# A two-layer decoder trunk on one core: tiles shifted so that matmul operands begin at multiples of 512 bytes, and the order inside the attention heads changed

## The chip, the core and the metric

The kernel runs on one core of a Trainium2 chip, and the metric is the device time of one execution in microseconds. The engines work side by side: TensorE (PE in the profile; its weight loads are a row of their own, PEld), VectorE (DVE), ScalarE (ACT), GpSimd (POOL) and SyncE (SP), which issues DMAs. On-chip memory has 128 partitions. A tile takes the same range of bytes in each of its partitions, so every tile has a first byte in its partition, and every operand of a matmul begins at some byte there. A matmul has two operands: the **moving** one, whose columns stream through the array, and the **stationary** one, which a weight load puts into the array beforehand. In the profile's rows `acc<-xTh,w` names the output, then the moving, then the stationary tile.

## What is computed

512 tokens of width 1024 pass through two layers. The reference, cut to its frame:

```python
for i in range(DEPTH):
    if i % 2 == 0:
        m = hybrid_attention_mixer(x, ...)   # latent attention (8 heads) + block attention (8 heads)
    else:
        m = ssd_mixer(x, ...)                # state-space mixer, 32 heads in 4 groups
    x = layer_norm(DEEPNORM_ALPHA * x + m, ln_mix_g[i], ln_mix_b[i])
    f = conv_ffn(x, w_up, conv_w, conv_b, w_down)      # width 2816, gated
    x = layer_norm(DEEPNORM_ALPHA * x + f, ln_ffn_g[i], ln_ffn_b[i])
    x = x + jax.nn.sigmoid(x @ ple_w_gate[i]) * (p[i] @ ple_w_proj[i])
```

All values are float32. In the latent attention a head's key is 64 columns of its own and 32 rotary columns that all eight heads share.

## The kernel before

**Arithmetic.** Each float32 operand of a large product is split into a high part (rounded to a matmul format, by ACT) and the rest (by DVE): `split`, lines 71 to 76. `mm3` (lines 104 to 107) then issues three matmuls for each product: high by high (L105), high by low (L106), low by high (L107). They have 128 stationary columns and mostly 512 moving ones. A weight is loaded by a DMA on SP's queue into `raw` (three buffers), split into a `w` tile, and used once.

**Streams.** Nearly all of the time is a few long streams of `mm3`. In the up projections of the feed-forward layers and the input projections of the mixer (`up_a`, `proj_a`) the weights are stationary and the transposed activations `xTh`, `xTl` move: `acc<-xTh,w`. In the down projections the weights move and the hidden tiles `h` are stationary: `acc<-w,h`. The state-space mixer's output has `acc<-w,yT`; the gate of the per-layer embedding has `pg<-w,xTh`, with its weights in the pool `hp`. In the attention output the half from block attention is `wo<-w,ob` and the half from latent attention `om<-w,om`: the same loop over the same shapes, with the weights of `wo` in the pool `wp` and those of `om` in `qkp`.

**Where tiles begin.** Pools take their room in the order in which they are opened, and a pool's tiles follow each other. The tiles of one pool are multiples of 512 bytes long (2,048, 4,096, 16,384), so all of them begin at the same remainder of 512, which comes from the small constants and statistics laid before them; and slices for matmuls step in multiples of 512 bytes. In the kernel before, `rawp`, `wp`, `xp`, `sp` and `tp` (weights `w`, tokens, scratch, `xTh`, `xTl`) have remainder 96; `c4`, `qkp`, `ptp`, `prp`, `big` and `hp` (keys and queries, `cT`, `pT`, `ob`, `om`, `h`, the weights of `pg` and `om`) have 224; `two`, `three` and `cvp` of the mixer (`yT`, `xdt`, `state`) have 64. So the two operands of a matmul begin at: `acc<-xTh,w` 96 and 96; `acc<-w,h` and `wo<-w,ob` 96 and 224; `pg<-w,xTh` 224 and 96; `om<-w,om` 224 and 224; `acc<-w,yT` 96 and 64.

**The heads.** The sixteen heads run as eight pairs, p = 0 to 7, the latent ones from p = 4. PE's order there is written by hand: at each p two pieces of `scores` (L329, tile `s`), then `turn` of the pair before (transposes of its weights, L356, tile `pt`), then `values` (L368, tile `o`); the table `between` puts other products into four gaps. `kr_step` makes the shared rotary key, `c_transpose` and `c_split` the split latent vectors `cT`, `v_step` (`vm`) and `uq_step` (`uq`) values and queries, and `ready` a pair's keys and queries (`mla_k`: `mk`, `mla`: `mq`). A scheduler that simulates the engines orders ACT, DVE, POOL and SP; `issue_after` holds a block of its work behind a named instruction.

Of the kernel before, what the change touches and what calls it, by code (L numbers as in the profile page):

```python
# [10 lines left out]
F32 = mybir.dt.float32  # L11
F32R = mybir.dt.float32r
I32 = mybir.dt.int32
AF = mybir.ActivationFunctionType
# [19 lines left out]
def trunk(ctx, tc, I, out):  # L34
# [9 lines left out]
    def pool(name, bufs, **kw):  # L44
        return ctx.enter_context(tc.tile_pool(name=name, bufs=bufs, **kw))
# [7 lines left out]
    st = pool("st", 4)  # L53
    pa = [pool(f"pa{i}", 2, space=PSUM) for i in range(2)]
# [16 lines left out]
    def split(h, l, src, eng=V, hi=A):  # L71
        if hi is A:
            A.activation(h, src, AF.Copy)  # L73
        else:
            hi.tensor_copy(h, src)
        eng.tensor_tensor(l, src, h.bitcast(F32), op=OP.subtract)  # L76
# [37 lines left out]
    qg = cp.tile([P, 3], F32, name="qg")  # L114

# [158 lines left out]
    def attention():  # L274
        with ExitStack() as es:
# [208 lines left out]
            def mla_k(j):  # L484
                ps = acc("mk", 1)
                w = L["wkv"][0][:, :, j * P:(j + 1) * P]
                mm3(ps, w[:, 0], w[:, 1], cT[2][:, 0], cT[2][:, 1], True, True)
                for x in range(2):
                    y = qkp.tile([P, 2, 512], F32R, tag="qk", name="mk")
                    split(y[0:64, 0], y[0:64, 1], ps[64 * x:64 * x + 64])  # L490
                    nc.scalar.dma_start(y[64:96].bitcast(F32), L["kr"].bitcast(F32))
                    mk[2 * j + x] = y
# [27 lines left out]
            def pj_load(half, *pools):  # L520
                L["pj"] = PleProj([(0, half)], *pools)
# [19 lines left out]
            def ready(p):  # L541

                if p >= 4:
# [9 lines left out]
                       3: ([(pp, 0, 0, 2), (pp, 0, 0, 3)], [(ct, 2), (ct, 0), (ct, 1), (kr_step,), (cs, 2), (cs, 0), (cs, 1)],  # L553
                           [(uq_load, 1), (vm, 0), (uq, 0, 0)],
                           [(uq, 0, 1), (uq, 0, 2), (uq, 0, 3), (vm, 1), (vm, 2), (uq, 1, 0), (ready, 4), (vm, 3)]),
                       4: ([(uq, 1, 1), (out_load, 0)], [(uq, 1, 2)], [(ready, 5), (uq, 1, 3)],
# [202 lines left out]
    def ssd(xs, xT):  # L759
        with ExitStack() as es:  # L760
# [6 lines left out]
            cvp = lpool("cvp", 2)  # L767
            cw = one.tile([P, 24, 5], F32, name="scw")
# [256 lines left out]
            ones = one.tile([P, P], F32, name="ones")  # L1025
            G.memset(ones, 1.0)
            b2 = bank("le")
            T.matmul(b2[:, :P], ones, da, start=True, stop=True)
# [121 lines left out]
```

## Time and profile before

| | us |
|---|---|
| median of 3 runs | 1468.15 (1464.94 to 1468.96) |
| the profiled execution | 1466.06 |
| its span, first to last instruction | 1464.3 |
| PE busy | 1452.5 |
| DVE busy | 855.5 |
| ACT busy | 656.4 |

The span is the time from the first instruction to the last; 1.8 us of the profiled execution lie around it. A matmul's own duration in the rows holds the filling and draining of the array and overlaps that of the next; what a matmul costs in a stream is the distance from its start to the next start.

### The profile page before, as it was taken

Reading aid. Unit: us, or ns where it says so; the run is one execution under the profiler, and the core shown is the slowest. Engines: PE = TensorE matmul, PEld = TensorE weight load, DVE = VectorE, ACT = ScalarE, POOL = GpSimd, SP = SyncE. Lnnn points to the kernel's source line nnn. Section 1 sums busy time; section 2 is a strip of 40 time slices with the busy share of each in tenths; the row PEclk is TensorE's granted clock in tenths of the full one; section 3 lists DMA queues with packets and bytes.
Section 4 is the critical chain, followed back from the end, with each engine's and each line's share of the span. In section 5 each row is a group of like instructions: output and inputs, shape, how many; then the busy total and the mean of one; then the engine's idle time right before and its main releaser. Section 6 shows DMA issues by size and latency. Waiting matters only on the chain.

```text
span 1464.3 us, 19196 instructions
## 1 busy us (share of the span) xinstructions
PE 1452.5 (99%) x7264; PEld 1194.8 (82%) x7264; DVE 855.5 (58%) x1499; ACT 656.4 (45%) x1273; POOL 138.1 (9%) x235
## 2 busy tenths in 40 slices
PE   9999999999999999999999999999999999999998
PEld 7876878888888888889888788787888888888887
DVE  5367787545445334756576877768854445423472
ACT  5476654534343322345756565463354333322331
POOL 2133313000000000100121201112100000000010
PEclk9999999999999999999999999999999999999999
DMA  6304133332333233332434333433333333232511
GB/s 236 112 30 155 59 112 110 101 101 92 97 100 101 89 99 129 131 118 76 140 109 130 103 114 108 130 108 116 96 117 95 97 101 101 87 101 86 174 49 51
DMA packets 51932, 155.93 MB, mean 106 GB/s; under 512 B 6400, under 2 KB 13312, under 8 KB 51840
## 3 DMA queue, kind: packets, MB, share of 16 engines
q1 hardware_dynamic: 39168, 135.49, 29.1%
q10 hardware_dynamic: 12672, 19.21, 4.1%
q8 instruction: 57, 0.93, 0.3%
q14 instruction: 35, 0.29, 0.1%
HBM read 148.26 MB, written 5.37 MB: 105 GB/s over the span
## 4 chain that ended last, share of the span: by engine, by line
PE 96%; DVE 2%; ACT 1%; DMA 1%; issue 0%; ACTq 0%; SPq 0%
PE acc L105 25%; PE acc L106 25%; PE acc L107 25%; PE pg L107 2%; PE pg L106 2%; PE pg L105 2%; PE s L329 2%; PE intra L915 1%; PE xTb L136 1%; PE pt L356 1%; PE o L368 1%; PE state L929 1%; PE inter L915 1%; PE wo L105 1%; PE om L105 1%; PE wo L107 1%
## 5 line engine op out<-in xcount | busy, mean ns | idle before, releaser
L76 DVE TENSOR_TENSOR w<-raw,w 128x512 fp32r<-128x512 f32 (+1 forms) x438 | 297.4, 689 | 282.1 <-ACT w L73 281.6
L73 ACT ACTIVATE w<-raw 128x512 fp32r<-128x512 f32 (+1 forms) x438 | 268.4, 625 | 403.0 <-PE acc L107 354.1
L106 PE MATMUL acc<-xTl,w 128*128 128x512 f32 (+1 forms) x1104 | 413.8, 375 | 0.8 <-DVE xTl L76 0.8
L105 PE MATMUL acc<-xTh,w 128*128 128x512 f32 (+1 forms) x1104 | 413.5, 376 | 0.2 <-ACT xTh L73 0.2
L107 PE MATMUL acc<-xTh,w 128*128 128x512 f32 (+1 forms) x1104 | 413.0, 374 | 0.0
L106 PEld LDWEIGHTS acc<-xTl,w 128*128 128x128 f32 x1104 | 207.9, 188 | 38.3 <-DVE xTl L76 1.2
L107 PEld LDWEIGHTS acc<-xTh,w 128*128 128x128 f32 x1104 | 207.8, 188 | 37.4 <-issue 0.6
L105 PEld LDWEIGHTS acc<-xTh,w 128*128 128x128 f32 x1104 | 207.4, 188 | 38.0 <-issue 1.1
L106 PE MATMUL acc<-w,h 128*128 128x512 f32 x352 | 139.1, 395 | 0.0
L107 PE MATMUL acc<-w,h 128*128 128x512 f32 x352 | 138.7, 395 | 0.0
L105 PE MATMUL acc<-w,h 128*128 128x512 f32 x352 | 138.5, 395 | 0.0
L607 DVE SCALAR_TENSOR_TENSOR conv<-acc,cw,conv 128x511 f32<-128x511 f32 x88 | 65.7, 746 | 87.2 <-ACT conv L605 87.2
L127 POOL TENSOR_TENSOR mv<-rs,half_neg 128x1 f32<-128x1 f32 x16 | 13.9, 869 | 760.8 <-DVE rs L126 760.8
L106 PEld LDWEIGHTS acc<-w,h 128*128 128x128 f32 x352 | 66.3, 188 | 15.5
L105 PEld LDWEIGHTS acc<-w,h 128*128 128x128 f32 x352 | 66.3, 188 | 15.3
L107 PEld LDWEIGHTS acc<-w,h 128*128 128x128 f32 x352 | 66.3, 188 | 15.3
L605 ACT ACTIVATE conv<-acc,cw 128x512 f32<-128x512 f32 x44 | 34.3, 780 | 83.6 <-PE acc L107 83.6
L631 DVE TENSOR_TENSOR conv<-conv,acc 128x512 f32<-128x512 f32 x44 | 30.3, 688 | 59.8 <-PE acc L107 57.3
L607 DVE SCALAR_TENSOR_TENSOR cv<-acc,scw,cv 128x511 f32<-128x511 f32 (+2 forms) x72 | 53.4, 744 | 15.4 <-ACT cv L605 14.8
L106 PE MATMUL pg<-w,xTh 128*128 128x512 f32 (+1 forms) x136 | 52.2, 384 | 0.0
L105 PE MATMUL pg<-w,xTh 128*128 128x512 f32 (+1 forms) x136 | 52.1, 384 | 0.0
L107 PE MATMUL pg<-w,xTl 128*128 128x512 f32 (+1 forms) x136 | 52.1, 383 | 0.0
(287 smaller groups left out, 2042.3 us busy)
## 6 DMA issues: line engine op xcount, KB each, us to landing
raw<-in_w_up SPq DMA_DIRECT2D x88, 512.0 KB, 3.5
raw<-in_w_down SPq DMA_DIRECT2D x44, 512.0 KB, 3.5
raw<-in_w_xbc SPq DMA_DIRECT2D x24, 512.0 KB, 3.5
raw<-in_w_ple_gate SPq DMA_DIRECT2D x16, 512.0 KB, 4.6
raw<-in_w_z SPq DMA_DIRECT2D x16, 512.0 KB, 3.5
lab<-rows ACTq DMA_DIRECT2D x16, 512.0 KB, 5.3
raw<-in_w_sout SPq DMA_DIRECT2D x16, 512.0 KB, 3.5
raw<-in_w_qkv SPq DMA_DIRECT2D x11, 512.0 KB, 4.9
```

What stands on the lines that cost most here:

```text
L73: A.activation(h, src, AF.Copy)
L76: eng.tensor_tensor(l, src, h.bitcast(F32), op=OP.subtract)
L105: T.matmul(ps, lh, rh, start=start, stop=False)
L106: T.matmul(ps, lh, rl, start=False, stop=False)
L107: T.matmul(ps, ll, rh, start=False, stop=stop)
L136: T.transpose(b[:, k * P:(k + 1) * P], src[:, (half * 4 + k) * P:(half * 4 + k + 1) * P], ident)
L329: T.matmul(b[:, :e], q[:, ts], k[:, :e], start=n == 0, stop=n == len(qk) - 1)
L356: T.transpose(b[:, at:at + P], self.soft[x][2][i][:, t], ident)
L605: A.activation(f, ps, AF.Identity, bias=cw[:, taps:taps + 1], scale=cw[:, taps - 1:taps])
L607: V.scalar_tensor_tensor(f[:, k:], ps[:, :S - k], cw[:, taps - 1 - k:taps - k], f[:, k:], op0=OP.mult, op1=OP.add)
L631: V.tensor_tensor(g, g, pu, op=OP.mult)
L915: T.matmul(b[64 * x:64 * x + 64, k * P:(k + 1) * P], weights[:, h * 64:h * 64 + 64], moving(h), start=True, stop=True)
```

## The change

Three tiles that only take room are added (384 bytes behind the pool `st`, 416 among the constants, 128 in the mixer's pool `one`), each written once by POOL, and the mixer's `ones` shrinks from 128 to 8 columns, with a piece of scratch filled with ones in its place for one matmul. With that, `rawp`, `wp`, `xp`, `sp`, `tp`, `c4`, `qkp`, `ptp`, `prp`, `big`, `hp`, `two`, `three` and `cvp` all begin at a multiple of 512. The identity that moves in every transpose stays at remainder 128, and the column sums of the mixer's norm (`ss`) stay off a multiple.

In the heads, `kr_step` goes ahead of the `cT` transposes; one more `vm` is computed earlier and the last one later; in `mla_k` both high parts are issued before both low parts; and the load and split of the second embedding projection (`pj_load`) are held until the end of the transposes of pair 5.

```diff
+    G.memset(pool("pad", 1).tile([P, 96], F32, name="pad"), 0.0)
...
+    G.memset(cp.tile([P, 104], F32, name="pad0"), 0.0)
...
-                for x in range(2):
-                    y = qkp.tile([P, 2, 512], F32R, tag="qk", name="mk")
-                    split(y[0:64, 0], y[0:64, 1], ps[64 * x:64 * x + 64])
+                halves = [ps[64 * x:64 * x + 64] for x in range(2)]
+                ys = [qkp.tile([P, 2, 512], F32R, tag="qk", name="mk") for _ in range(2)]
+                for y, h in zip(ys, halves):
+                    A.activation(y[0:64, 0], h, AF.Copy)
+                for x, (y, h) in enumerate(zip(ys, halves)):
+                    V.tensor_tensor(y[0:64, 1], h, y[0:64, 0].bitcast(F32), op=OP.subtract)
                     nc.scalar.dma_start(y[64:96].bitcast(F32), L["kr"].bitcast(F32))
                     mk[2 * j + x] = y
...
             def pj_load(half, *pools):
-                L["pj"] = PleProj([(0, half)], *pools)
+                with tc.issue_after(pairs[5].last_a.ins) if half else ExitStack():
+                    L["pj"] = PleProj([(0, half)], *pools)
...
-                       3: ([(pp, 0, 0, 2), (pp, 0, 0, 3)], [(ct, 2), (ct, 0), (ct, 1), (kr_step,), (cs, 2), (cs, 0), (cs, 1)],
-                           [(uq_load, 1), (vm, 0), (uq, 0, 0)],
-                           [(uq, 0, 1), (uq, 0, 2), (uq, 0, 3), (vm, 1), (vm, 2), (uq, 1, 0), (ready, 4), (vm, 3)]),
-                       4: ([(uq, 1, 1), (out_load, 0)], [(uq, 1, 2)], [(ready, 5), (uq, 1, 3)],
+                       3: ([(pp, 0, 0, 2), (pp, 0, 0, 3)], [(kr_step,), (ct, 2), (ct, 0), (ct, 1), (cs, 2), (cs, 0), (cs, 1)],
+                           [(uq_load, 1), (vm, 0), (vm, 1), (uq, 0, 0)],
+                           [(uq, 0, 1), (uq, 0, 2), (uq, 0, 3), (vm, 2), (uq, 1, 0), (ready, 4), (uq, 1, 1)]),
+                       4: ([(uq, 1, 2), (out_load, 0)], [(vm, 3)], [(ready, 5), (uq, 1, 3)],
...
+            G.memset(one.tile([P, 32], F32, name="pads"), 0.0)
...
-            ones = one.tile([P, P], F32, name="ones")
+            ones = one.tile([P, 8], F32, name="ones")
             G.memset(ones, 1.0)
+            all_ones = w0[:, :P]
+            G.memset(all_ones, 1.0)
             b2 = bank("le")
-            T.matmul(b2[:, :P], ones, da, start=True, stop=True)
+            T.matmul(b2[:, :P], all_ones, da, start=True, stop=True)
```

What stands on DVE behind the scores of p = 3, where PE's next transposes wait for DVE's copies of `pt`. Before:

```order
L445 TENSOR_SCALAR cg<-ct,qg 128x512 x3
L75 CAST spare<-kr 32x512
L361 COPY pt<-pt 128x512
L76 TENSOR_TENSOR cT<-cg,cT 128x512 x2
L76 TENSOR_TENSOR spare<-kr,spare 32x512
L361 COPY pt<-pt 128x512
L76 TENSOR_TENSOR cT<-cg,cT 128x512
L76 TENSOR_TENSOR pT<-p_raw,pT 128x512
L361 COPY pt<-pt 128x512
```

After, on DVE at the same place:

```order
L77 CAST spare<-kr 32x512
L448 TENSOR_SCALAR cg<-ct,qg 128x512
L78 TENSOR_TENSOR spare<-kr,spare 32x512
L448 TENSOR_SCALAR cg<-ct,qg 128x512 x2
L364 COPY pt<-pt 128x512
L78 TENSOR_TENSOR cT<-cg,cT 128x512
L364 COPY pt<-pt 128x512
L78 TENSOR_TENSOR cT<-cg,cT 128x512
L364 COPY pt<-pt 128x512
```

Both roundings of the shared key (`spare<-kr`) now stand ahead of the first copy, one `cT` instead of two and a key behind it, and the split of `pT` is gone from here.

What stands on DVE between the weights of pair 4 and the scores of p = 5, where PE waits for the keys and queries `mk` and `mq` of pair 5. Before:

```order
L76 TENSOR_TENSOR mk<-mk 64x512
L76 TENSOR_TENSOR w<-raw,w 128x512
L76 TENSOR_TENSOR pT<-p_raw,pT 128x512
L76 TENSOR_TENSOR w<-raw,w 128x512
L76 TENSOR_TENSOR mk<-mk 64x512
L76 TENSOR_TENSOR mq<-mq 96x512 x2
L76 TENSOR_TENSOR ob<-o,ob 128x512
```

After, on DVE at the same place:

```order
L497 TENSOR_TENSOR mk<-mk 64x512 x2
L78 TENSOR_TENSOR mq<-mq 96x512 x2
L78 TENSOR_TENSOR w<-raw,w 128x512
L78 TENSOR_TENSOR ob<-o,ob 128x512
L335 ISA pr,nmx<-s,mask 128x512
```

The three weight and embedding splits no longer stand between the two keys; one weight split is left, behind the queries. On ACT the two `mk` rows stand together too, with the DMA of the shared key behind them.

## Rows read from the trace of the kernel before

**Rows 1.** The page: busy time by engine; the chain that ended last, by engine.

```profile
PE 1452.5 (99%) x7264; PEld 1194.8 (82%) x7264; DVE 855.5 (58%) x1499; ACT 656.4 (45%) x1273; POOL 138.1 (9%) x235
...
PE 96%; DVE 2%; ACT 1%; DMA 1%; issue 0%; ACTq 0%; SPq 0%
```

**Rows 2.** Windows: stretch, length, PE busy (instructions), clock, DMA share, GB/s.

```profile
280.00:380.00 100.00, 100.00 (x443) 1.00 0.30 95
...
490.00:590.00 100.00, 100.00 (x432) 1.00 0.37 121
```

**Rows 3.** Groups by line and shape: count | busy us, mean ns | idle before.

```profile
L105 PE MATMUL acc<-xTh,w 128*128 128x512 f32 x944 | 369.1, 391 | 0.0
...
L105 PE MATMUL acc<-w,h 128*128 128x512 f32 x352 | 138.5, 395 | 0.0
...
L105 PE MATMUL acc<-w,yT 128*128 128x512 f32 x128 | 51.1, 399 | 0.0
...
L105 PE MATMUL pg<-w,xTh 128*128 128x512 f32 x120 | 47.6, 398 | 0.0
```

**Rows 4.** Timeline of PE, up projection: start us, duration us, instruction.

```profile
299.80 0.39 PE L105 MATMUL acc<-xTh,w 128*128 128x512 f32 x1
...
302.07 0.39 PE L106 MATMUL acc<-xTl,w 128*128 128x512 f32 x1
```

**Rows 5.** Timeline of PE, down projection.

```profile
500.06 0.40 PE L105 MATMUL acc<-w,h 128*128 128x512 f32 x1
...
503.55 0.39 PE L105 MATMUL acc<-w,h 128*128 128x512 f32 x1
```

**Rows 6.** Timeline of PE, gate of the embedding, 512 columns.

```profile
640.20 0.39 PE L105 MATMUL pg<-w,xTh 128*128 128x512 f32 x1
...
642.30 0.40 PE L105 MATMUL pg<-w,xTh 128*128 128x512 f32 x1
```

**Rows 7.** Timeline of PE, output of the state-space mixer.

```profile
1026.12 0.39 PE L106 MATMUL acc<-w,yT 128*128 128x512 f32 x1
...
1030.79 0.39 PE L105 MATMUL acc<-w,yT 128*128 128x512 f32 x1
```

**Rows 8.** Timeline of PE, the two halves of the attention output.

```profile
161.53 0.39 PE L105 MATMUL wo<-w,ob 128*128 128x512 f32 x1
...
164.08 0.39 PE L107 MATMUL wo<-w,ob 128*128 128x512 f32 x1
...
214.82 0.39 PE L106 MATMUL om<-w,om 128*128 128x512 f32 x1
...
216.40 0.39 PE L107 MATMUL om<-w,om 128*128 128x512 f32 x1
```

**Rows 9.** Timeline of PE, last gate, 256 columns.

```profile
1454.82 0.28 PE L105 MATMUL pg<-w,xTh 128*128 128x256 f32 x1
...
1458.06 0.28 PE L105 MATMUL pg<-w,xTh 128*128 128x256 f32 x1
```

**Rows 10.** Waits of PE: waiting line <- releaser: us in total, times, longest.

```profile
PE s L329 <- ACT mq L73: 1.6, 2, 1.1
PE pt L356 <- ACT pt L359: 1.4, 1, 1.4
...
PE s L329 <- DVE mq L76: 0.7, 1, 0.7
PE pt L356 <- DVE pt L361: 0.5, 1, 0.5
```

**Rows 11.** Timelines of ACT and DVE in the heads, p = 3 to 5.

```profile
125.31 1.65 ACT L73 ACTIVATE cT<-cg 128x512 fp32r<-128x512 f32 x3
...
127.16 0.67 DVE L76 TENSOR_TENSOR spare<-kr,spare 32x512 fp32r<-32x512 f32 x1
...
156.65 0.68 DVE L76 TENSOR_TENSOR pT<-p_raw,pT 128x512 fp32r<-128x512 f32 x1
```

**Rows 12.** Windows, all engines, the middle of the heads: PE clock before DMA share.

```profile
100.00:146.00 46.00, 42.30 (x233) 32.69 (x232) 34.92 (x95) 31.19 (x79) 15.59 (x44) 0.96 0.37 123
```

**Rows 13.** Timeline at the start: POOL's memsets, PE's first stream.

```profile
0.73 0.52 POOL L287 MEMSET zero<- 128x512 f32 x1 [0.29 <-POOLq L1142]
1.19 0.42 POOL L119 MEMSET mask<- 128x384 f32 x1
...
5.52 0.50 PE L105 MATMUL acc<-w,xTh 128*128 128x512 f32 x1
```

## The prediction

> **What bounds the kernel now.** I read the page first: PE is busy for 99% of the span and holds 96% of the chain that ended last [rows 1]. Whatever is not on PE therefore counts only where PE waits for it. The waits of PE by name come next: those of the heads are 1.6, 1.4, 0.7 and 0.5 us [rows 10], and nothing comparable stands in the long streams. So the change can bring time in two ways only: fewer PE waits in the heads, or a shorter distance from one matmul's start to the next in the streams.
>
> The second is what the shifted tiles touch, so I looked for streams of equal shape with different distances. The windows show it at once: 100 us of up projection hold 443 matmuls, 100 us of down projection 432, both with the clock at 1.00 of its upper level, 2.4 GHz, and PE busy throughout [rows 2]. The timelines give the distances of matmuls with 512 moving and 128 stationary columns. Up projection: 10 starts in 2.27 us, 227.0 ns [rows 4]. Down projection: 15 in 3.49 us, 232.7 ns [rows 5]. Gate: 9 in 2.10 us, 233.3 ns [rows 6]. State-space output: 20 in 4.67 us, 233.5 ns [rows 7].
>
> Set beside where the operands begin (moving, stationary): 96 and 96 costs 227.0; 96 and 224 costs 232.7; 224 and 96 costs 233.3; 96 and 64 costs 233.5. These streams differ in more than that, so the pair that decides is the attention output, one loop over equal shapes whose two halves differ in the pool of the weights. `wo` (96 and 224) takes 11 starts in 2.55 us, 231.8 ns; `om` (224 and 224) takes 7 in 1.58 us, 225.7 ns, within the rounding of two starts the 227 of the up projection [rows 8]. **My reading:** a stream is short where both operands begin at the same remainder of 512, whichever that is, and 5 to 6.5 ns longer where they don't. After the change all of them begin at 0 and 0, which the trace does not show.
>
> **The change part by part. The shifted tiles.** If 0 and 0 behaves as 96 and 96 and as 224 and 224, the slow streams come to 227.0. Each of the counts stands for three lines [rows 3]:
> - down projections: 3 × 352 = 1,056 matmuls by 232.7 − 227.0 = 5.7 ns: 6.0 us;
> - state-space output: 384 by 6.5 ns: 2.5 us;
> - gates: 360 by 6.3 ns: 2.3 us;
> - `wo`: 96 by 4.8 ns: 0.5 us.
>
> The rest with unequal starts (`uq`, `vm`, some of `pj`; under 300, partly narrower) would give at most 1.5 us at the same rate; I take 0.5. The sum is 11.8 us, all on PE in streams in which it waits for nothing, so all of it is on the path. ACT and DVE are busy for 45% and 58% of the span [rows 1], so a stream 2.5% faster should not be starved.
>
> The bounds of the unknown, what 0 and 0 costs: the nearest rows are the two equal pairs (227.0 and 225.7 by rounding), which give nothing off or up to a nanosecond for all streams, and the three unequal ones (up to 233.5), which would be a loss. I take 227.0, because two different equal pairs lie there, and no row of an equal pair lies at 232. Below, a floor comes from the narrow gate: with 256 columns, 27 starts take 3.24 us, 120.0 ns [rows 9]. From 256 to 512 columns a matmul of the equal pairs thus grows by 107 ns, so 512 columns alone are 214 ns and 13 ns are a fixed part, whose origin no row tells.
>
> The Trainium skill ("TensorE: Matmul & The Clock Gate", Step-by-step: what each phase is for) says that PE reads SBUF through two independent read ports, one for the streaming operand and one for the weights. By that rule two operands could not get into each other's way, where they begin would be without effect, and only the heads would gain (the second rival). The trace speaks against it: `wo` and `om` differ by 6 ns with nothing else changed [rows 8].
>
> **The heads.** PE's order is by hand, so I follow who waits for whom. Pair 5: the scores `s` wait for ACT's and DVE's `mq` because DVE works on two weight splits and one split of `pT` between the two `mk` (the order rows; the `pT` split is 0.68 us [rows 11]), and ACT's second `mk` waits behind the same splits. With these gone the keys and queries are ready about 2 us sooner, more than the waits. Pair 4: ACT's second `mk` follows the first at once, and two `uq` products in place of one `vm` cover more of the wait. Both waits of `s`, 1.6 + 0.7 us [rows 10], go: −2.3 us. What comes late next is PE itself.
>
> Ahead of that, at p = 3, the picture is mixed. The first copy of `pt` on DVE now stands behind one more split of the shared key (0.67 us [rows 11]), so the transposes that waited 0.5 us wait up to 0.6 us longer. ACT's copy stands behind two `cT` instead of three (1.65 us for three [rows 11]), which takes some 0.5 us off the 1.4 us wait. I count it as zero, with +0.6 and −1.4 as ends. In this stretch the granted clock is 0.96 [rows 12], which is 4% of 46 us, 1.8 us, at most to be had back if PE's pause no longer lets it fall to 1.2 GHz; I take none, and +0.9 as the other end, if the pause gets longer. Sum of the heads: −2.3, between −5.5 and +1.5.
>
> `pj_load` is held until the transposes of pair 5 are through. What waits for it are the last `pj` products, behind the attention output; two splits of `pT` and the weight splits move into the pairs 6 and 7, where DVE and ACT are free between the pieces. SP's queue gets one load of `raw` later; no weight of pair 6 is behind it. Zero, and 0.7 us if one split should hold a PE step.
>
> **The added memsets.** Two stand ahead of the zero fill that starts PE's warm-up. The 512-column fill starts 0.46 us before the next one [rows 13]; two of about a fifth of that are 0.2 us. PE's first stream, at 5.52 us, follows right on the warm-up, so I add 0.1 (0 to 0.25). The fill of ones for the mixer is one POOL step in a stretch where POOL is idle (9% busy [rows 1]): zero.
>
> **Sum.** 1466.1 − 11.8 − 2.3 + 0.1 = 1452.1 for an execution like the profiled one, which is 2.1 us under the median of the runs; against the median that is **1454**.
>
> **The rivals.**
> 1. *The fixed part goes too.* The 13 ns beyond the columns might be what it costs that operands begin off some boundary: all streams of before begin at 96, 224 or 64, never at 0. The four streams of rows 3 hold 3 × (944 + 352 + 128 + 120) = 4,632 matmuls; half to all of 13 ns is 30 to 60 us more, 1424 to 1394. For it: nothing in the trace begins at 0. Against it: 96, 224 and 64 are three different remainders, and the fixed part is never smaller than in the equal pairs. The Trainium skill ("TensorE: Matmul & The Clock Gate", Back-to-back issue gap) gives a warm distance of N / 2.4 + 2.5 ns, 215.8 ns for 512 columns, without a word on where operands begin; by it, as an estimate from that page, 11.2 ns would go and the time would be near 1402. No row of before reaches it.
> 2. *The place does not matter.* The streams differ for another reason (which tile is stationary, which engine wrote it last), and only the heads change: 1466.1 − 2.2 + 2.1 = 1466. The pair `wo` and `om` speaks against it.
> 3. *Equal starts at 0 collide.* Slower: if both operands begin in the same place of the 512 bytes and that place is the bad one, the up projections and their like, 3 × 944 = 2,832 matmuls at 227.0, go to the 233.5 of the slowest pair: +18.4 us, while the slow streams stay: 1466.1 + 18.4 − 2.2 + 2.1 = 1484. It decides from the distance at which the streams together break even with all that is gained: (11.3 − 0.5 + 2.2) / 4,632 = 2.8 ns above 227.0, so from 229.8 ns on. Against it: two equal pairs, both short.
>
> **How the numbers follow.** The forecast 58%, rival 1 17%, rival 2 13%, rival 3 12%. 0.3% of the time, 4.4 us, is about what a measurement of this kernel can tell from no change: 1463.8 to 1472.6 counts as the same. Forecast and rival 1 are faster: 0.75; rival 2 is the same: 0.13; rival 3 is slower: 0.12. The forecast's own range is 1446 to 1464: streams 1 ns shorter than 227.0 (about 5 us) with 3 us more from the heads, to streams 1 ns longer with the heads at their bad end. The range reaches up to the other cases, 1446 to 1486, and leaves out rival 1.
>
> **What would show it.** In the profile after: 100 us of down projection should hold as many matmuls as 100 us of up projection, 443, and the gate and state-space output should start every 227 ns (right), all streams at 216 to 222 (rival 1), the differences unchanged (rival 2), or all near 233 (rival 3). The waits of `s` for `mq` should be gone from the list, those of `pt` stay at about 2 us, and the clock of the middle of the heads at 0.96 or above. I am wrong altogether if the distance depends on something that the tiles' shift changes besides the remainder, such as which tiles are neighbours.

## The result and the profile after

The changed kernel takes **1451.1 us** (median of 4 runs, 1450.7 to 1451.8) against 1468.6 us for the kernel before in the same comparison (1464.9 to 1469.4): a ratio of 0.9888, 95% interval 0.9873 to 0.9902. It is faster, as the interval lies below 1, and within 3 us of the forecast. The runs of before spread over 4.4 us, which the section on the clock takes up. The profiled execution took 1451.2 us with a span of 1449.4, 14.9 us less than the span before.

The page after, busy time of PE and the chain by engine; they answer to [rows 1]:

```profile
PE 1440.7 (99%) x7264; PEld 1193.0 (82%) x7264; DVE 854.2 (59%) x1499; ACT 655.8 (45%) x1273; POOL 139.8 (10%) x239
...
PE 93%; DVE 4%; DMA 1%; ACT 1%; issue 1%; POOL 0%; DVEq 0%; ACTq 0%; POOLq 0%
```

PE is still the bound: the same 7,264 matmuls, 11.8 us less of busy time. Windows of PE after, up projection and then down projection (length, busy and count, clock, DMA share, GB/s), beside [rows 2]:

```profile
280.00:380.00 100.00, 100.00 (x443) 1.00 0.31 95
490.00:590.00 100.00, 100.00 (x442) 1.00 0.41 135
```

Down projection went from 432 to 442 matmuls in 100 us; up projection did not change. Timeline of PE after, the first and the last row of a stretch of down projection, of gate and of state-space output, as in [rows 5 to 7]:

```profile
500.03 0.39 PE L108 MATMUL acc<-w,h 128*128 128x512 f32 x1
...
503.43 0.39 PE L108 MATMUL acc<-w,h 128*128 128x512 f32 x1
...
640.36 0.40 PE L109 MATMUL pg<-w,xTl 128*128 128x512 f32 x1
...
642.41 0.39 PE L109 MATMUL pg<-w,xTl 128*128 128x512 f32 x1
...
1010.09 0.39 PE L107 MATMUL acc<-w,yT 128*128 128x512 f32 x1
...
1012.82 0.39 PE L107 MATMUL acc<-w,yT 128*128 128x512 f32 x1
```

15 starts in 3.40 us are 226.7 ns, 9 in 2.05 are 227.8, 12 in 2.73 are 227.5. All three slow streams came down to the distance of the up projection, none below it.

The heads. Waits of PE after (beside [rows 10]):

```profile
PE warm L293 <- POOL zero L290: 1.6, 1, 1.6
PE acc L108 <- DVE xTl L78: 0.8, 1, 0.8
PE pt L359 <- DVE nmx L335: 0.8, 2, 0.4
PE mq L505 <- DVE spare L274: 0.6, 1, 0.6
PE uq L107 <- ACT v L410: 0.4, 1, 0.4
PE s L332 <- DVE mq L78: 0.2, 1, 0.2
```

Of the 2.3 us in which `s` waited for `mq`, 0.2 are left. Both waits of `pt` for its copies (1.4 and 0.5 us) are gone too, and two small waits are new (0.6 and 0.4). The middle of the heads, all engines, PE's clock before the DMA share, beside [rows 12]:

```profile
100.00:146.00 46.00, 44.07 (x256) 34.71 (x256) 36.45 (x103) 32.41 (x85) 18.10 (x50) 1.00 0.36 124
```

PE gets 256 matmuls into these 46 us where it got 233, and the clock is 1.00 for 0.96.

To see where the 14.9 us lie, I set start times of the same matmul side by side. From the first scores (74.7 us) to the last product of `om`, the end of the heads, 4.9 us are gained. The shift between the traces then stays at 4.7 us through the up projection and grows by 3.0 over the down projection, 1.0 over the gate, 2.2 over the mixer, 0 over the second up projection, 3.0 over the second down projection and 0.9 over the last gate: 10.1 us behind the heads. Of the mixer's 2.2 us some 0.35 belong to the new heads and not to the streams: they come at 1050 us, where a group of transposes (`xTb`, of the norm behind the mixer) stands earlier on PE, in all six kernels with the new heads and not with the fills alone, which gain 9.8 us behind the heads. The first 75 us are 0.25 us longer.

### The profile page after: what moved, and what is told of

The parts are those of the page before. It is cut to its first block, busy times and chain, and to the rows that moved or that the text cites. A ratio compares the mean times of both kernels' runs of the same rounds, so it can differ in the third digit from the quotient of the medians.

```text
span 1449.4 us, 19202 instructions
## 1 busy us (share of the span) xinstructions
PE 1440.7 (99%) x7264; PEld 1193.0 (82%) x7264; DVE 854.2 (59%) x1499; ACT 655.8 (45%) x1273; POOL 139.8 (10%) x239
## 4 chain that ended last, share of the span: by engine, by line
PE 93%; DVE 4%; DMA 1%; ACT 1%; issue 1%; POOL 0%; DVEq 0%; ACTq 0%; POOLq 0%
PE acc L108 24%; PE acc L107 24%; PE acc L109 24%; PE pg L109 2%; PE pg L107 2%; PE pg L108 2%; PE s L332 2%; PE xTb L139 1%; PE intra L924 1%; PE pt L359 1%; PE o L371 1%; PE state L938 1%; PE inter L924 1%; PE om L107 1%; DVE w L78 1%
## 5 line engine op out<-in xcount | busy, mean ns | idle before, releaser
L108 PE MATMUL acc<-w,h 128*128 128x512 f32 x352 | 137.1, 390 | 0.0
L109 PE MATMUL acc<-w,h 128*128 128x512 f32 x352 | 136.8, 390 | 0.0
L107 PE MATMUL acc<-w,h 128*128 128x512 f32 x352 | 136.6, 389 | 0.0
```

The costliest lines, as they stand in the source:

```text
L107: T.matmul(ps, lh, rh, start=start, stop=False)
L108: T.matmul(ps, lh, rl, start=False, stop=False)
L109: T.matmul(ps, ll, rh, start=False, stop=stop)
```

## The experiments

Spans and heads of the kernels in one table. "Heads" is the time from the first scores to the start of the last `om` product, as a difference from the first profiled execution of the kernel before (169.5 us). "Falls" counts the stretches of the heads in which the granted clock of the profiled execution was at its lower level; one such stretch is worth about 1.6 us (the section on the clock; the longest, with the hold alone, about twice that), so rows compare well only where this number is the same.

| kernel | median us (ratio, 95%) | span us | heads us | falls |
|---|---|---|---|---|
| before | 1468.6 | 1464.3 | 0 | 1 |
| before, profiled again | 1464.5 (one run) | 1462.7 | -1.9 | 0 |
| after | 1451.1 (0.9888, 0.9873 to 0.9902) | 1449.4 | -4.9 | 0 |
| new heads, no fills | 1461.5 (0.9964, 0.995 to 0.9979) | 1459.5 | -4.7 | 0 |
| fills, old heads | 1455.8 (0.9927, 0.991 to 0.9943) | 1454.7 | -0.1 | 1 |
| all at 96 | 1451.2 (0.9896, 0.988 to 0.9911) | 1448.7 | -5.0 | 0 |
| upper pools at 256 | 1451.8 (0.99, 0.9883 to 0.9916) | 1448.6 | -5.3 | 0 |
| `mk` order alone | 1463.2 (one run) | 1461.4 | -3.3 | 0 |
| hold of `pj` alone | 1471.1 (one run) | 1469.3 | +5.2 | 3 |
| table alone | 1464.9 (one run) | 1463.1 | -1.3 | 1 |
| after without the hold | 1451.7 (0.9892, 0.9874 to 0.991) | 1450.3 | -5.0 | 0 |
| after with a later `pj` | 1454.2 (0.9914, 0.9898 to 0.993) | 1452.4 | -2.1 | 0 |

The kernel before ran again in each comparison, with medians of 1465.3 to 1468.8; the ratios are against its runs in the same comparison.

### The two halves apart

The heads alone:

```diff
-    G.memset(pool("pad", 1).tile([P, 96], F32, name="pad"), 0.0)
...
-    G.memset(cp.tile([P, 104], F32, name="pad0"), 0.0)
...
-            G.memset(one.tile([P, 32], F32, name="pads"), 0.0)
...
+            ones = one.tile([P, P], F32, name="ones")
```

> The changed kernel without its four fills, so that every tile lies where it lay before; the new order of the heads stays. Theory (the two halves of the change add up): the heads stage alone is worth what the start times of the changed kernel show there, 4.9 us; 1468.6 - 4.9 = 1463.7 us, the clock in 100 to 146 us stays at 1.00, the transposes no longer wait for the copies of `pt`, and down projection stays at about 432 matmuls in 100 us. Rival (the heads gained because the products in them became shorter too): 2.3 us as the prediction had it, 1466.3 us, with the clock back at 0.96 and the `pt` waits back at 1 us or more.

The fills alone (the heads as before):

```diff
-                       3: ([(pp, 0, 0, 2), (pp, 0, 0, 3)], [(kr_step,), (ct, 2), (ct, 0), (ct, 1), (cs, 2), (cs, 0), (cs, 1)],
+                       3: ([(pp, 0, 0, 2), (pp, 0, 0, 3)], [(ct, 2), (ct, 0), (ct, 1), (kr_step,), (cs, 2), (cs, 0), (cs, 1)],
...
-                with tc.issue_after(pairs[5].last_a.ins) if half else ExitStack():
-                    L["pj"] = PleProj([(0, half)], *pools)
+                L["pj"] = PleProj([(0, half)], *pools)
```

> The fills alone, with the heads in their old order. Theory: the streams alone, about 10.2 us by the start times: 1458.4 us; down projection, gate and state-space output at 227 to 228 ns, the heads' waits and their clock of 0.96 as before. Rival (the streams gained because something of the heads' order, such as the later load of `pj`, moved transfers away from them): the streams stay at 232 to 233 ns and the time is within 2 us of 1468.

The window of PE in down projection (490 to 590 us), with the heads alone:

```profile
490.00:590.00 100.00, 100.00 (x432) 1.00 0.38 127
```

and with the fills alone:

```profile
490.00:590.00 100.00, 100.00 (x443) 1.00 0.39 124
```

The heads alone gain 4.8 us of span and leave the streams at 432; the fills alone gain 9.6 and leave the waits of the heads as they were. The product of the ratios, 0.9891, is that of the whole change: the halves add up. The fills shortened the streams, not the later load of `pj`. The theory held for both in the waits and the streams. Its 0.96 for the clock with the fills alone did not come: it was 1.00 there, and it fell later, at pair 5 (the section on the clock). Both times came out 2 to 3 us under what was expected; that had been worked out from a kernel before at 1468.6 us, and in this comparison it took 1465.3.

### What counts: the place or the difference of places

All tiles 96 behind a multiple of 512, by one wider pad:

```diff
-    G.memset(cp.tile([P, 104], F32, name="pad0"), 0.0)
+    G.memset(cp.tile([P, 128], F32, name="pad0"), 0.0)
```

> The changed kernel with the lower pad 24 elements wider (128 for 104 columns), so that all tiles of all pools, weights, moving operands and stationary ones alike, begin 96 bytes behind a multiple of 512. Theory A (only the difference of the two starts counts): same as the changed kernel, 1451 us, 227 ns in all streams. Theory B (it is the multiple of 512 that helps): the 4,632 products of the four streams lose the 5 to 6 ns again, 1451 + 4,632 x 0.0055 = 1476 us; by a weaker form of B only the streams that were slow before lose it, 1461 us.

The upper pools at 256, the lower ones at 0:

```diff
-    G.memset(pool("pad", 1).tile([P, 96], F32, name="pad"), 0.0)
+    G.memset(pool("pad", 1).tile([P, 160], F32, name="pad"), 0.0)
```

> The changed kernel with the upper pad 64 elements wider (160 for 96 columns): the tiles of the upper pools (`h`, `yT`, `pg`'s moving operand, the heads' tiles, the small ones) begin at 256 behind a multiple of 512, those of the lower pools (weights, `xTh`) at 0. Up projection keeps equal starts. Theory A with a period of 512 bytes: down projection, gate and state-space output go back to about 232.5 ns, 1451 + 10 = 1461 us, while up projection stays at 227. Theory A with a period of 256 bytes or less (a half of 512 is as good as the whole): 1451 us, 227 ns everywhere. Theory C (it grows with the distance between the two remainders, and 256 is the largest): more than 233 ns, 1463 us or above.

The same window with all at 96:

```profile
490.00:590.00 100.00, 100.00 (x443) 1.00 0.42 136
```

and with the upper pools at 256:

```profile
490.00:590.00 100.00, 100.00 (x443) 1.00 0.41 133
```

Both are as fast as the changed kernel. So a multiple of 512 has no merit of its own (96 and 96 does as well), and the period is 256 bytes at most: 0 and 256 count as equal. Multiples of 512 are more than is needed.

### A ruler for the distance

Two kernels that hold nothing but streams of 48 matmuls; the first, and the second with other pairs. The format to which `split` rounds its parts, and in which the matmuls of the kernel run, is called fp32r (four bytes); the ruler has streams in bf16 (two bytes) beside it:

```diff
+    def stream(name, m, s, n=512, cols=128, half=False, count=16):
+        for i in range(count):
+            q = [s // size + 256 * (i % 2) + 128 * j for j in range(2)]
+            r = [m // size + 512 * j for j in range(2)]
+            for k, (a, b) in enumerate([(q[0], r[0]), (q[0], r[1]), (q[1], r[0])]):
+                T.matmul(ps[:cols, :n], stt[:, a:a + cols], mt[:, b:b + n], ...)
```

> None of the trunk is computed. PE runs streams of 48 products, each stream twice, out of one tile of moving and one of stationary operands, both fp32r and both beginning at a multiple of 512 bytes; the slices taken of them begin so and so many bytes behind that, as the names say (m_zero_s_thirtytwo: moving at 0, stationary at 32). In each stream two slices of each operand alternate as in the kernel, and nothing else runs beside it. Theory A (equal remainders of 256 bytes are needed, whatever the remainder): 227 ns with moving at 0 for stationary at 0 and 256, and for the equal pairs 16/16, 64/64, 96/96, 128/128; 231 to 234 ns for every other pair, 96/224, 224/96, 96/64, 0/128 among them. Theory B (equal remainders of a smaller power of two, 64 or 32, are needed, and something else of the tiles made 96/224 slow in the kernel): 0/64, 0/128, 0/192 and 96/224 at 227 ns. Theory C (the distance grows with the difference of the remainders): a rise from 0/4 over 0/16 and 0/32 to its largest at 0/128, and a fall behind it. Of the fixed 13 ns: if it belongs to fp32r, the streams in bf16 come nearer to 213 ns; if it belongs to every product, they stay at 227.

> Again only streams of 48 products, each twice, with other starts; none of the trunk is computed. In the first such kernel the equal pairs 0, 64, 96 and 128 took 227 ns and so did 0/256, 0/192 took 229, all other unequal pairs 231.5 to 234, and the equal pair 16/16 took 231 and 233. Theory A (equal remainders of 256 help where they are multiples of 32 or more): 32/32, 160/160, 192/192, 224/224, 96/352 and 224/480 at 227; 4/4, 8/8, 16/16, 48/48 and 16/272 at 231 or above. Theory B (16/16 was late for how its stream began): these at 227 too. For a stationary operand 192 ahead of the moving one: 229 at every such pair (32/224, 64/256, 96/288, 128/320) if the difference counts alone, more at some if not; 64/0 and 192/0 (which are 192 and 64 ahead, modulo 256) at 229 and 233. Stationary operands of 96 and 112 columns: 227 like 128 if only the starts count, 230 like 64 columns if it is the length of the read that has to fit. With one and the same stationary slice, or one and the same moving slice, no change if the starts alone count. In the mixed stream two thirds of the products have equal starts: 227 for these and 233 for the others, 229 in the mean, if each product counts by itself.

Timeline of PE in the first ruler; each row is one stream, so the distance to the next row's start over 48 is the distance of its matmuls (names too long for the column lose their beginning):

```profile
25.14 11.05 PE L74 MATMUL m_zero_s_zero<-mv,sv 128*128 128x512 f32 x48
36.03 11.32 PE L74 MATMUL m_zero_s_four<-mv,sv 128*128 128x512 f32 x48
47.19 11.36 PE L74 MATMUL m_zero_s_sixteen<-mv,sv 128*128 128x512 f32 x48
...
92.01 11.32 PE L74 MATMUL m_zero_s_onetwentyeight<-mv,sv 128*128 128x512 f32 x48
103.17 11.37 PE L74 MATMUL m_zero_s_onesixty<-mv,sv 128*128 128x512 f32 x48
114.37 11.16 PE L74 MATMUL m_zero_s_oneninetytwo<-mv,sv 128*128 128x512 f32 x48
125.37 11.36 PE L74 MATMUL m_zero_s_twotwentyfour<-mv,sv 128*128 128x512 f32 x48
136.56 11.05 PE L74 MATMUL m_zero_s_twofiftysix<-mv,sv 128*128 128x512 f32 x48
147.45 11.31 PE L74 MATMUL m_zero_s_threeeightyfour<-mv,sv 128*128 128x512 f32 x48
...
347.02 10.54 PE L74 MATMUL bf_s_zero<-mb,sb 128*128 128x512 bf16 x48
357.39 10.52 PE L74 MATMUL bf_s_thirtytwo<-mb,sb 128*128 128x512 bf16 x48
367.75 10.52 PE L74 MATMUL bf_s_sixtyfour<-mb,sb 128*128 128x512 bf16 x48
```

The first row: 36.03 - 25.14 = 10.89 us for 48, 226.9 ns; the second 11.16, 232.5; bf16 at 0: 10.37, 216.0. All streams of both rulers, worked out in this way, from the first of the two times that each is run (fp32r where nothing else is said):

| moving / stationary begins at | ns from start to start |
|---|---|
| 0/0, 0/256, 64/64, 96/96, 128/128 | 226.9, 226.9, 227.3, 227.3, 227.7 |
| 32/32, 160/160, 192/192, 224/224, 96/352, 224/480 | 227.5, 227.7, 227.5, 227.3, 227.5, 227.1 |
| 96/224, 224/96, 96/64 (the pairs of the kernel before) | 232.3, 232.3, 233.3 |
| 0/4, 0/16, 0/32, 0/64, 0/96, 0/128 | 232.5, 233.3, 233.1, 233.3, 234.0, 232.5 |
| 0/160, 0/224, 0/384, 0/480, 16/0, 32/0, 128/0, 192/0 | 233.3, 233.1, 232.3, 233.3, 231.7, 233.3, 233.3, 233.1 |
| stationary 192 ahead: 0/192, 32/224, 64/256, 96/288, 128/320, 64/0 | 229.2 at 0 in the first ruler; all six 228.8 to 229.0 in the second |
| equal, no multiple of 32: 4/4, 8/8, 16/16, 48/48, 16/272 | 237.5, 232.1, 230.0 to 231.3, 230.0, 231.3 (the second time 16/16 231.0 and 233.1, 48/48 231.0, 16/272 233.3) |
| 0/0, stationary of 112, 96, 64, 32 columns | 229.2, 230.2, 230.0, 231.7 |
| 0/128, stationary of 64, 32 columns | 229.4, 230.4 |
| moving of 416, 384, 256, 128 columns: at 0/0; at 0/128 | 188.5, 173.3, 120.0, 110.4; 189.8, 175.8, 118.5, 111.9 |
| one stationary slice only; one moving slice only: 0/0; 0/128 | 226.9, 226.9; 232.3, 232.3 |
| a third of the products at 0/128, the rest at 0/0 | 231.3 |
| bf16: 0/0, 0/32, 0/64, 0/128 | 216.0, 215.8, 215.8, 215.8 |

The kernel's three pairs come out within 1 ns of what its streams showed. Theory A of the first ruler held, with two limits that I had not foreseen: the starts have to be multiples of 32 bytes as well (theory A of the second), and a stationary operand that begins 192 bytes ahead, modulo 256, costs only 2 ns and not 6, wherever the moving one begins. There is no growth with the difference (theory C falls). In the mixed stream the mean is 231.3 ns, where 229 were expected if each matmul counts by itself. Its start times show why: of the three distances in each round, the one between the two equal matmuls is 226.9, and both that touch the unequal one are long, 232.7 up to its start and 234.0 behind it. So an unequal matmul among equal ones is paid for twice.

The fixed part: with the same shape and clock, bf16 takes 216 ns and fp32r 227. Of the 13 ns over the columns (512 at 2.4 GHz are 213.3), 11 belong to fp32r, and in bf16 none of the four starts tried changes anything.

The Trainium skill ("TensorE: Matmul & The Clock Gate", Back-to-back issue gap) gives N / 2.4 + 2.5 ns for a matmul by itself at the upper clock, as an estimate from it 215.8 for 512 columns; the bf16 streams agree to 0.2 ns, the fp32r streams of this kernel do not. The same page (Step-by-step: what each phase is for) says that the two operands are read through independent ports, by which where they begin should not matter; in bf16 the ruler agrees, in fp32r it measures 227 or 233 ns by the starts alone. Why fp32r differs, no run here shows.

### The heads, part by part

Each part was put alone into the kernel before. The order of `mk`:

```diff
-                for x in range(2):
-                    y = qkp.tile([P, 2, 512], F32R, tag="qk", name="mk")
-                    split(y[0:64, 0], y[0:64, 1], ps[64 * x:64 * x + 64])
+                for y, h in zip(ys, halves):
+                    A.activation(y[0:64, 0], h, AF.Copy)
+                for x, (y, h) in enumerate(zip(ys, halves)):
+                    V.tensor_tensor(y[0:64, 1], h, y[0:64, 0].bitcast(F32), op=OP.subtract)
```

> The kernel before with one part of the new heads: the two high parts of `mk` come ahead of the two low ones. Theory (the key's rounding is what the scores wait for): the waits of `s` for `mq` (1.6 us for ACT, 0.7 us for DVE) shrink by 1 us or more, the waits of `pt` stay (1.4 and 0.5), the clock in 100 to 146 us stays at 0.96; the span is shorter by 1 to 2.3 us, 1462.0 to 1463.3. Rival (ACT and DVE are late because of the weight splits ahead of `mk`, whichever order its halves have): the waits stay within 0.5 us, span 1464.3.

The hold of `pj`:

```diff
-                L["pj"] = PleProj([(0, half)], *pools)
+                with tc.issue_after(pairs[5].last_a.ins) if half else ExitStack():
+                    L["pj"] = PleProj([(0, half)], *pools)
```

> The kernel before with only the load of `pj` held until the transposes of pair 5. Theory as predicted (it moves splits to where nobody waits): the span as before, 1464.3 within 0.5 us. Rival (its splits of `pT` and of weights are what stands ahead of `mk` on ACT and DVE): the waits of `s` for `mq` fall from 2.3 us to under 1 us and the span falls by as much, 1462.5 or less.

The table:

```diff
-                       3: ([(pp, 0, 0, 2), (pp, 0, 0, 3)], [(ct, 2), (ct, 0), (ct, 1), (kr_step,), (cs, 2), (cs, 0), (cs, 1)],
-                           [(uq_load, 1), (vm, 0), (uq, 0, 0)],
+                       3: ([(pp, 0, 0, 2), (pp, 0, 0, 3)], [(kr_step,), (ct, 2), (ct, 0), (ct, 1), (cs, 2), (cs, 0), (cs, 1)],
+                           [(uq_load, 1), (vm, 0), (vm, 1), (uq, 0, 0)],
```

> The kernel before with only the new order of the products in the pairs 3 and 4 (shared key first, the `vm` earlier). Theory, as the traces since the prediction suggest (the bank of `kr` comes free early, so the five transposes of `pt` have four banks in place of three): both waits of `pt` (1.4 and 0.5 us) go, the clock in 100 to 146 us is 1.00 in place of 0.96, the span is 2.5 to 3.7 us shorter, 1460.6 to 1461.8, and the waits of `s` for `mq` stay at about 2 us. Rival, the prediction's account (the `pt` waits only shift from one engine to the other): the waits of `pt` stay at 1 us or more, the clock at 0.96, the span within 1 us of 1464.3.

**`mk` order.** Waits of PE for the keys and queries in this kernel:

```profile
PE s L329 <- DVE mq L76: 0.8, 1, 0.8
...
PE s L329 <- ACT mq L73: 0.3, 1, 0.3
```

The 2.3 us became 1.1, as the theory had it. The span, 1461.4, lies under its range, because the clock, expected at 0.96, was 1.00: against the execution of before without a fall (1462.7, the last experiment) the order of `mk` gains 1.3 us.

**Hold of `pj`.** Its waits of `s`, and windows of PE (length, busy and count, clock, DMA share, GB/s):

```profile
PE s L329 <- ACT mq L73: 1.6, 2, 1.1
...
PE s L329 <- DMA mk<-spare: 0.7, 1, 0.7
PE s L329 <- DVE mq L76: 0.7, 1, 0.7
```

```profile
126.00:132.00 6.00, 4.74 (x17) 0.72 0.88 335
144.00:152.00 8.00, 7.27 (x26) 0.57 0.03 6
195.00:200.00 5.00, 5.00 (x18) 0.66 0.14 52
```

Both expectations fall; this execution lost 5.0 us. At pair 5, where the splits stood, 1.2 us are gained. They now stand ahead of the last `mk`, and of the waits above 1.1 us fall there, at 193 us. Why the transfer of the shared key into `mk` came 0.7 us late at 145 us, no run here settles. Most of the loss is the clock. It fell to its lower level, 1.2 GHz, three times: behind the waits of `pt`, as in the execution of before, behind the waits of `s` at 142 to 145 us, and behind those at 193. As an estimate, the length of each window times what its clock lacks of 1.00, the three cost 6.8 us, against 1.7 for the one of before: 5.1 us more. With one execution, and a clock that falls in one execution and not in another (the last experiment), what the hold costs by itself is not shown.

**Table.** Its waits, and PE's window behind the first of them:

```profile
PE s L329 <- DVE mq L76: 1.4, 1, 1.4
...
PE uq L105 <- ACT v L407: 0.9, 1, 0.9
...
PE mq L498 <- DVE spare L271: 0.6, 1, 0.6
```

```profile
157.00:162.00 5.00, 5.00 (x18) 0.66 0.38 152
```

The waits of `pt` went, as expected, and the clock from 100 to 146 us was 1.00. But `s` waits 1.4 us for `mq` at pair 5, the clock fell right behind that (0.66), and the span gained 1.2 us where 2.5 to 3.7 were expected. Like for like, with one fall in either execution, the table is thus worth 1.2 us and, with no fall in either, the order of `mk` 1.3: together 2.5 of the 3.0 us that the new heads gain on the execution without a fall.

Why the waits of `pt` went is read from the timelines of the kernel after, first PE, then DVE:

```profile
121.77 0.61 PE L460 MATMUL kr<-cst,hc 128*32 128x128 f32 x4
122.22 1.47 PE L446 MATMUL ct<-cst,hc 128*128 128x128 f32 x12
123.81 3.17 PE L359 MATMUL pt<-cst,pr 128*128 128x128 f32 x20
```

```profile
123.68 0.67 DVE L78 TENSOR_TENSOR spare<-kr,spare 32x512 fp32r<-32x512 f32 x1
```

The table alone took these waits away, the order of `mk` alone and the hold alone left them. The transposes write into a pool of four tiles in PSUM, called banks (`pb`). A bank is free when its last reader is through, and `kr`'s last reader is the second half of its split. Before, that ended at 127.8 us [rows 11], so the five `pt` had three banks between them, and the last had to wait for ACT's copy. Now it ends at 123.68 + 0.67 = 124.35, all four banks are in use, and the 20 transposes run without a wait that the list shows. The fifth `pt` starts at 126.32 in the kernel after, right behind the first copy of `pt` (DVE, to 126.27), and at 127.49 in the kernel before, right behind the second (ACT, to 127.44).

### The hold inside the whole change, and a later load

```diff
-                with tc.issue_after(pairs[5].last_a.ins) if half else ExitStack():
-                    L["pj"] = PleProj([(0, half)], *pools)
+                L["pj"] = PleProj([(0, half)], *pools)
```

> The changed kernel without the hold of the load of `pj`; everything else stays. With the load held and nothing else changed, the kernel before lost 5.0 us of span, because its splits then stood ahead of the last `mk` and not of an earlier one, and the clock fell in both places. Theory (the hold moves about the same wait from one pair to another): the wait of `s` for `mq` at about 187 us goes (0.3 us), a wait of 0.5 to 1 us comes back at about 155 us; span 1449.4 + 0.2 to 0.7, time within 1 us of 1451. Rival 1 (the hold is a loss in the changed kernel too): no wait at 155 us, span 1449.1 or less. Rival 2 (the hold carries the gain of the heads): the waits of `s` come back with 1.5 us or more and the clock falls, 1453 us or above.

```diff
-                with tc.issue_after(pairs[5].last_a.ins) if half else ExitStack():
+                with tc.issue_after(pairs[6].last_a.ins) if half else ExitStack():
...
-                       6: ([(wo, 0, 2)], [], [(ready, 7), (wo, 0, 3)], [(pj_load, 1, c4, "c4", wp, "w")]),
+                       6: ([(wo, 0, 2)], [], [(ready, 7), (wo, 0, 3)], []),
...
+        G.memset(pad, 0.0)
+        G.memset(pad0, 0.0)
```

> The changed kernel with two things put off: the load of `pj` stands behind the products of the last pair and is held until that pair's transposes are through, and the two fills that make room are done behind PE's warm-up (the room itself stays). Theory: the wait of `s` for `mq` at about 187 us (0.3 us) goes, the first stream starts 0.25 us sooner, span 1449.4 - 0.5 = 1448.9, which no comparison of whole times can tell from 1449.4, only the start times. Rival: the last `pj` products now wait for their weights at about 222 us, by up to the 2.4 us that the splits take, span 1449.4 to 1451.5.

Without the hold the heads take 5.0 us less than before, with it 4.9: nothing, once the order of `mk` and of the table are there; its first 75 us were 0.9 us longer in that execution, which makes its longer span. The wait at 155 us that the theory wanted did not come back (rival 1's mark), but one did at 129 us, where PE waits for ACT's `v` longer than the 0.4 us of the kernel after:

```profile
PE uq L107 <- ACT v L410: 0.9, 1, 0.9
```

The table alone, which has no hold either, has the same 0.9. About 0.35 us are won back without the hold at 185 to 190 us. So the hold moves a short wait from one place to another, as the theory said, and gains nothing in sum. The later load was a loss of 3 us; ACT's timeline in that kernel tells why, and PE's after it:

```profile
207.14 1.15 ACT L75 ACTIVATE pT<-p_raw 128x512 fp32r<-128x512 f32 x2 [0.83 <-DMA p_raw<-in_pT]
208.19 0.58 ACT L364 ACTIVATE pt<-pt 128x512 f32<-128x512 f32 x1
```

```profile
208.82 0.44 PE L361 MATMUL pt<-cst,pr 128*128 128x128 f32 x2 [2.17 <-ACT pt L364]
```

ACT stands waiting for a load (0.83 us) with the copy of `pt` queued behind, and PE's transposes wait 2.17 us for that copy. The rival was right on the loss, but wrong on the place and too low. With the two fills behind it the warm-up starts at 1.31 us, as in the kernel before, in place of 1.56; what that is worth at the end cannot be told, as the first 75 us of these kernels scatter by over a microsecond.

### The clock

The kernel before, unchanged:

> The kernel before itself, once more. In its profiled execution the clock fell to 0.67 to 0.76 between 126 and 132 us, behind the two waits of `pt`; in the kernels with the fills alone and with the new order of `mk` alone the same two waits stood there and the clock stayed at 1.00. Theory (at waits of this length the clock falls in one execution and not in the next): the waits are again 1.4 and 0.5 us, and the clock may be 1.00 this time, the span then 1464.3 - 1.6 = 1462.7. Rival (the clock's fall belongs to this program): the same 0.7 there, the same span within 0.5 us. One execution can show that the clock stays; if it falls again, nothing is settled.

The window 126 to 132 us of PE (busy, count, clock) in the profiled execution of the section on the time before:

```profile
126.00:132.00 6.00, 4.63 (x19) 0.72 0.92 352
```

and in this one:

```profile
126.00:132.00 6.00, 4.63 (x29) 1.00 0.93 363
```

The waits are the same (1.4 and 0.5 us), and in both PE had done nothing but transposes since 122 us, with these waits between them; the clock was 0.72 in one execution and 1.00 in the other, and the span 1464.3 and 1462.7, as the theory had it. With the fills alone and with `mk` alone it was 1.00 too, with the hold alone 0.72: lower in two executions of five. And with the fills alone it fell at pair 5 (157 to 162 us), behind the same waits of `s` at which it stayed at 1.00 in both executions of the kernel before:

```profile
157.00:162.00 5.00, 4.27 (x15) 0.76 0.68 231
```

So at pauses like these the clock falls in one execution and not in another.

Other executions agree. Of the 19 of the kernel before whose mean clock is on record, eight have 1.000 and took 1464.4 to 1465.8 us, six have 0.996 and took 1468.4 to 1469.7, and five lie between. Of the 26 of kernels with the new heads, none is under 0.999. So the new heads gain more than their waits: in these executions the falls no longer come either. Between executions without a fall the whole change is worth 13.3 us (1464.5 and 1451.2); the other 4 us between the medians are as much as lies between executions at 1.000 and at 0.996.

## Why the prediction was right, and where it was off

**The streams: right in mechanism, 1.8 us too much.** The reading from `wo` and `om` that a stream is short where both operands begin at the same remainder is what the two shifted kernels and the ruler show; it is a remainder of 256 and not of 512. That nothing else parts `wo` and `om` was argued there; the ruler, which changes only the starts, shows it. Down projection gave 6.0 us, as summed. The gates gave 1.9 for 2.3, the mixer 1.8 for 2.5, `wo` about 0.3 for 0.5, and of the 0.5 for the rest nothing is seen. Two steps are mis-sized. One is the 227.0 for every stream: a stream that has just been interrupted needs some matmuls to find its distance (in the pieces of `wo` and `om` after the change the first three to ten distances mostly lie at 228 to 236 ns), so the means over all start times, the interruptions left out, are 227.9 for `yT` and 228.7 for `wo`, whose pieces are short. The other is the distance before, taken from one short stretch each: over the whole streams the means are 233.1 and not 233.5 for `yT`, 232.8 and not 233.3 for the gates.

**The heads: 4.9 us for 2.3.** Against the execution of before in which the clock did not fall, the gain is 4.9 - 1.9 = 3.0 us. The waits add up to the same: `s` 2.1 and `pt` 1.9 gone, 0.6 and 0.4 new; the 0.3 of `wo` would come on top and is within what these sums are good for. Two steps failed. The waits of `pt`, counted as zero, followed the order of the copies on DVE and ACT and missed what the transposes wait for, a bank: 1.9 us went, 0.5 more than the lower end of -1.4. And the clock was put at 0 with 1.8 us as the end: the end came, but only since the execution shown had a fall that others have not. The upper end of the sum, +1.5, holds only if none of the 2.3 us comes; with it the terms named there give -0.8.

**Hold of `pj`: right that it is nothing in the changed kernel, not shown in the reason.** It was put "where DVE and ACT are free between the pieces"; alone it makes PE wait 1.1 us for the last queries, at 193 us. That it does not in the changed kernel fits the new order of `mk`, in which the keys no longer stand behind the splits; no run has the hold together with the order of `mk` alone.

**The fills:** the warm-up starts 0.25 us later for the 0.1 taken, at the bound, and less than the starts scatter.

**From the profiled execution to the median:** 14.9 us came in the spans for 14.0 forecast, and without the fall in the execution of before 13.3. That this is near is in part luck, as 1.8 us too much in the streams stand against about 0.7 too little in the heads. The other 2 us are the offset of 2.1 us that I carried over from the runs of before. This step failed: the offset belonged to them, as their times go with their mean clock (1464.4 to 1465.8 us at 1.000, 1468.4 to 1469.7 at 0.996), while all four runs after have 1.000 and lie within 1.1 us of each other.

**The rivals.** Rival 1 falls: the 13 ns stayed at 0/0, and the bf16 streams show whose they are. Rival 2 falls with the fills alone, rival 3 with 442 matmuls where it had them unchanged at 432 and up projection slower.

## What to carry to other kernels

Where fp32r matmuls run back to back with 512 moving and 128 stationary columns, let both operands begin at the same remainder of 256 bytes, a multiple of 32: here 6 ns of 233 in each matmul, bought with a pad of a few hundred bytes. Look for it by counting matmuls in equal windows of streams of equal shape. In a hand-ordered stretch ask of each PSUM bank who reads it last, and before you judge a part of a change by one execution, compare the clock of its windows: the hold alone seemed to lose 5 us, and that is about what its falls of the clock cost more than the one of before.

## What the runs showed of the hardware that I had not expected

- In fp32r the start of one operand against the other is worth 6 ns of 227 with 512 moving columns, 2.5 with 384, 1.3 with 416 and nothing with 256 (120.0 and 118.5); in bf16 nothing. One unequal matmul among equal ones lengthens the distance on both its sides.
- Fewer stationary columns do not help: 96, 64 and 32 columns with equal starts take 230 to 232 ns, against 227 for 128; 64 and 32 at 0/128 take 229 and 230. Fewer moving columns stop helping below 256: 128 take 110 ns, 256 take 120.
- Equal starts that are no multiple of 32 bytes lose much or all of the gain: 16/16 and 48/48 take 230 to 233 ns, 8/8 232, and 4/4 is the slowest of all, 237.5.
- The clock fell to 0.72 of a 6 us window in one execution of a kernel and stayed at 1.00 in the next, with the same waits; one such fall is 1.6 us of the span here.
